# A planner-ordered decoder layer: other first loads, one-row products for a scale, two additions on GpSimd, and a new table of shifts

## The chip, the cores and the metric

The kernel runs on one core of one Trainium2 chip. The metric is the device time of one execution in microseconds (us). Three executions of the kernel before took 1163.86, 1164.89 and 1165.84 us, so the time before is their median, 1164.89 us.

The engines are named as in the profile: PE is TensorE (PEld its weight loads), DVE is VectorE, ACT is ScalarE, POOL is GpSimd, and SP is the queue of SyncE, from which nearly all transfers are started.

## The reference, cut to what matters

One decoder layer on a sequence of 1024 rows of width 1024, in float32. In shortened form:

```python
c_act = silu(c)
sh1, sc1, g1, sh2, sc2, g2 = split(c_act @ w_mod + b_mod, 6)   # six vectors of 1024
h = rms_norm(x, norm_mix_w) * (1 + sc1) + sh1
proj = h @ w_in                        # lx, ly (512 each), q, k, v, z (4 heads x 128 each), beta, alpha
# group 1: gated recurrence over lx, four blocks of 128 channels
xr = conv4(lx);  r, i = sigmoid(block products of xr)
h_lru = scan(a(r), sqrt(1 - a^2) * i * xr)
out_lru = rms_norm(h_lru * gelu(ly), lru_norm_w)      # needs the sum of squares over all four blocks
# group 2: gated delta rule, 4 heads, chunks of 64 rows
q, k, v = silu(conv4(q, k, v));  T = inverse(I + strict_lower(beta k k^T decay))
o = chunked recurrence;  out_gdn = rms_norm(o, gdn_norm_w) * silu(z)
x = x + g1 * (concat(out_lru, out_gdn) @ w_out)
h = rms_norm(x, norm_mlp_w) * (1 + sc2) + sh2
x = x + g2 * (square(relu(h @ w_up)) @ w_down)        # 1024 -> 4096 -> 1024
out = rms_norm(x, final_norm_w)
```

## The kernel before, in words

Every product that needs float32 exactness is done as three products of split operands: an operand is rounded to the type fp32r ("high"), the rest is kept in a second tile ("low"), and high x high, high x low and low x high are summed in PSUM (`mm3`, L596). Tiles are 128 partitions by 1024 columns (512 KB); 43 of them share the buffers of `big`. PSUM has 8 banks.

The work runs in stages, which the profile shows one behind the other.

1. **Start (0 to about 60 us).** The first loads are `x` (eight tiles `x0` to `x7`), the columns of `w_mod` that make the scale (`sc_w`), and the key columns of `w_in` (`wk`). `scale1(q)` (L864) makes a quarter of the scale, 256 of its 1024 values: eight blocks of `w_mod` are multiplied by the eight columns of `c_act` and added up, the first on ACT and seven on DVE (`macc`, L668), and PE then sums the 128 partitions with two products against a column of ones (tile `sc_c`). `xnorm(t)` (L833) normalises a row block of `x`. PE transposes it (`xTq`, `xTp`), ACT and DVE scale and split it into `hh` and `hl`, and the products for the four key heads follow (`first`, L797, tile `k_p`). The planner runs 36 products into a tile called `warm` (L900), which nobody reads.
2. **Projections z, q, v (to about 350 us)**, in three column groups of 342 each (`Proj.third`, L770), and beside them the keys' `LT` tiles, the triangular inverse, and the chunked recurrence of each head (`chain`, L1216).
3. **The inverse (`inverse`, L1064)**: a forward substitution of 31 steps on DVE, then `level1` (tiles `it` and `iy`, 32x32 products) and `level2` (tiles `iw` and `iz`, 64x64 products). Between `iy` and `iw`, DVE writes tile `aw`; `iw` needs it.
4. **Recurrence (about 300 to 465 us)**: `lx`, `ly` and `lru` (L1304), one block of 128 channels after the other. The low half of the convolved `xr`, tile `xrl`, is made in three steps: ACT rounds `xr` into `xrh`, ACT writes its negative into `xrl`, and a transfer issued from POOL's queue adds `xr` to it in memory (`GD`, the class `Adder`, L512). The `gate` products need `xrl`. The sum of squares over the four blocks, `msum`, is gathered in the same way: ACT squares a block into `lsq`, and a transfer from POOL's queue adds it to `msum`. The products `lrus` read `msum`.
5. **Output projection (tiles `wg`, `wl`), then the MLP**: `up` (tiles `upx`, `upy`, `upz`) and the down products (tile `dn`), to the end. The MLP uses seven products in place of eight.

What sets the order: nothing runs in the order of the source. A `Recorder` (L184) collects some 8370 operations, and `schedule` (L248) plays them once through a model of the engines with durations written in the code, and emits them in the order that comes out. Each engine and the SP queue then work in that fixed order. An operation's rank is `op.pri` (L258): for operations of the backbone (`rec.bb`) and all others it is the latest start that the model allows; for the early ones (`rec.early`) it is their place in the list. To this the planner adds a hand of tuned shifts: the table `SHIFTS` (L130) holds one small integer for each recorded operation, in quarters. In the early part the rank is therefore

```python
op.adj = SHIFTS[len(self.ops)] / 4.0
op.pri = i - 1e5 + op.adj      # early operations; lowest rank first
```

Operations with the bias `FILL` come last among those that are ready: PE takes one only when the model has nothing else for it. The model's durations for the small products of the inverse stand in L48: `L1A_DUR` 0.12 and `L1B_DUR` 0.2 us for one group of `level1`, `L2_DUR` 0.14 us for one of `level2`. A transfer that adds is modelled with `ADD_LAT` 1.8 us and 195 KB per us.

## Time and profile before

| what | value |
|---|---|
| median of three runs | 1164.89 us (1163.86 to 1165.84) |
| the profiled execution's own time | 1164.92 us |
| its span (first to last instruction) | 1162.9 us |
| mean granted TensorE clock | 0.984 |
| PE busy | 1129.3 us |
| DVE, ACT, POOL busy | 800.4, 635.3, 268.9 us |
| moved by the DMA engines | 250.03 MB |

How to read it: about 2 us of the time lie outside the span. The row by engine gives busy time; a busy PE says only that some product was in flight, so it has to be read beside the granted clock, which halves in places. The rows by stretch (one row for each stretch of time: its length, then the busy time and number of instructions of PE, PE's weight loads, DVE, ACT and POOL, then the granted clock, the share of the 16 DMA engines and their GB/s) show where that is. A row of the timeline gives start, duration, engine, line, operation, the tile written and the tiles read; the bracket is how long the engine had been idle and who ended that.

### The profile page before, as it was taken

How to read it: one execution, taken by the hardware profiler on the slowest of the kernel's cores; microseconds unless marked ns; L12 is line 12 of the kernel's file. 1: busy time of each engine (PE TensorE's matmuls, PEld its weight loads, DVE VectorE, ACT ScalarE, POOL GpSimd, SP SyncE). 2: the span in 40 equal slices, each digit the busy share in tenths (PEclk: the TensorE clock that was granted, in tenths of full speed). 3: DMA queues.
4: the chain of work that ended last, by engine and by line, in shares of the span. 5: the costliest groups of instructions: out<-in, count | busy, mean ns of one | idle time of the engine just before them, and what ended most of it. 6: DMA issues, size and time to landing. Idle time of an engine off the chain costs nothing.

```text
span 1162.9 us, 16590 instructions
## 1 busy us (share of the span) xinstructions
PE 1129.3 (97%) x6224; PEld 974.9 (84%) x6224; DVE 800.4 (69%) x1136; ACT 635.3 (55%) x982; POOL 268.9 (23%) x188
## 2 busy tenths in 40 slices
PE   5999997999998999899999999999999999999999
PEld 4889997899998987677888888887888888888888
DVE  7746799559767669757866666767675474974563
ACT  5746735454648895467655555556645343443341
POOL 2202210211211233200013121214500085723030
PEclk9999998699999999899999999999999999999999
DMA  9848955449667293522278777775999767774631
GB/s 335 263 112 256 295 174 170 140 124 275 193 170 211 65 295 107 168 82 87 91 253 276 242 252 265 241 236 202 387 390 402 272 211 272 269 252 132 227 134 73
DMA packets 135332, 250.03 MB, mean 215 GB/s; under 512 B 11282, under 2 KB 56527, under 8 KB 135251
## 3 DMA queue, kind: packets, MB, share of 16 engines
q1 hardware_dynamic: 130786, 232.71, 57.5%
q0 software_dynamic: 4464, 16.25, 7.3%
q8 instruction: 49, 0.80, 0.3%
q14 instruction: 33, 0.26, 0.1%
HBM read 173.93 MB, written 58.74 MB: 200 GB/s over the span
## 4 chain that ended last, share of the span: by engine, by line
PE 86%; DVE 5%; ACT 4%; DMA 3%; issue 2%; POOL 0%; SPq 0%; POOLq 0%; DVEq 0%; ACTq 0%
PE dn L414 27%; PE upx L414 15%; PE upz L414 8%; PE k_p L414 4%; PE z_p L414 4%; PE q_p L414 4%; PE upy L414 4%; PE wl L414 4%; PE v_p L414 3%; PE lx_p L414 2%; PE ch L414 2%; PE ly_p L414 2%; DVE xr L414 1%; PE cho L414 1%; DMA sc_w<-in_w_mod_dram 1%
## 5 line engine op out<-in xcount | busy, mean ns | idle before, releaser
L414 PE MATMUL upx<-h2h,U 128*128 128x512 f32 x512 | 167.8, 394 | 0.0
L414 PEld LDWEIGHTS upx<-h2h,U 128*128 128x128 f32 x512 | 96.2, 188 | 22.6
L414 PE MATMUL upx<-h2l,U 128*128 128x512 f32 x256 | 100.8, 394 | 0.0
L414 POOL TENSOR_TENSOR wd<-wd,wd 128x512 f32<-128x512 f32 x32 | 45.6, 1427 | 233.1 <-DMA wd<-in_w_down_dram 187.8
L414 ACT ACTIVATE act<-act 128x512 f32<-128x512 f32 x112 | 70.8, 633 | 51.1 <-DVE act L414 48.9
L414 DVE TENSOR_TENSOR U<-wu,U 128x512 fp32r<-128x512 f32 x112 | 78.1, 714 | 15.9 <-ACT U L414 15.8
L414 PE MATMUL upz<-h2h,U 128*128 128x512 f32 x256 | 85.0, 394 | 0.0
L414 ACT CAST U<-wu 128x512 fp32r<-128x512 f32 x112 | 66.7, 617 | 22.0 <-DVE wu L414 10.6
L414 DVE TENSOR_TENSOR act<-upz,ek 128x512 f32<-128x512 f32 x32 | 22.1, 691 | 55.9 <-PE upz L414 35.9
L414 PEld LDWEIGHTS upx<-h2l,U 128*128 128x128 f32 x256 | 48.1, 188 | 11.5
L414 PEld LDWEIGHTS upz<-h2h,U 128*128 128x128 f32 x256 | 48.1, 188 | 11.3
L414 ACT COPY ek<-upx 128x512 f32<-128x512 f32 x48 | 28.1, 586 | 53.5 <-PE upx L414 50.3
L414 PE MATMUL upz<-h2l,U 128*128 128x512 f32 x128 | 50.5, 395 | 0.0
L414 POOL TENSOR_TENSOR R<-R,R_5o 128x1024 f32<-128x1024 f32 x8 | 22.1, 2778 | 91.7 <-DVE keep L414 85.2
L414 PE MATMUL upy<-h2h,U 128*128 128x512 f32 x128 | 43.0, 394 | 0.0
L414 DVE TENSOR_TENSOR wu<-wu,wu 128x512 f32<-128x512 f32 x48 | 36.7, 779 | 0.0
L414 ACT ACTIVATE vn<-ch,bcoef 128x128 f32<-128x128 f32 x32 | 11.6, 366 | 44.1 <-PE ch L414 44.1
L414 PE MATMUL k_p<-hh,wkh 128*128 128x256 f32 (+2 forms) x104 | 30.9, 327 | 1.4 <-ACT hh L414 1.4
L414 PE MATMUL lx_p<-hl,lx_wh 128*128 128x342 f32 x96 | 32.1, 334 | 0.0
L414 PE MATMUL lx_p<-hh,lx_wl 128*128 128x342 f32 x96 | 32.0, 333 | 0.0
L414 PE MATMUL lx_p<-hh,lx_wh 128*128 128x342 f32 x96 | 31.7, 330 | 0.0
L414 PE MATMUL q_p<-hh,q_wl 128*128 128x342 f32 x96 | 31.5, 328 | 0.0
(578 smaller groups left out, 3578.8 us busy)
## 6 DMA issues: line engine op xcount, KB each, us to landing
L<-aod SPq DMA_DIRECT2D x56, 512.0 KB, 6.8
R<-in_w_down_dram SPq DMA_DIRECT2D x40, 512.0 KB, 6.1
wu<-in_w_up_dram SPq DMA_DIRECT2D x32, 512.0 KB, 4.0
aod<-as SPq DMA_DIRECT2D x64, 256.0 KB, 2.3
wd<-in_w_down_dram SPq DMA_DIRECT2D x32, 512.0 KB, 6.7
aod<-act SPq DMA_DIRECT2D x48, 256.0 KB, 2.2
sc_w<-in_w_mod_dram SPq DMA_DIRECT2D x16, 512.0 KB, 8.2
x<-in_x_dram SPq DMA_DIRECT2D x16, 512.0 KB, 6.3
```

The lines of the kernel that those rows point to most:

```text
L414: op.fn(*[res(v) for v in op.a], **{n: res(v) for n, v in op.k.items()})
```

## The change

The change has six parts.

1. **The first loads get another order.** In the source `x1` moves ahead of the second half of the first quarter of the scale, and the blocks for quarters two and three of the scale are loaded as four tiles of 512 columns (two quarters at once). Their final order on the SP queue comes from the new table (part 6).
2. **Part of the scale by one-row products.** Quarters 0 and 1 of the scale no longer use ACT and DVE: PE multiplies each of the eight columns of `c_act` (as a weight of one column) with a block of 256 columns and sums the eight in PSUM as one row (`sc1_r`); DVE copies the row, and PE turns it into two columns with two products against a single one. Quarters 2 and 3 become one pass of 512 columns in two groups of four blocks, one on ACT and three on DVE in each.
3. **The `warm` products move to the front.** The same 36, now `ones` by `ones`, are recorded first; the first of them has an early rank, and the other 35 keep the bias `FILL`.
4. **`xnorm`**: the scaling of `x2`, `x4` and `x6` moves from DVE to ACT.
5. **Two accumulating transfers become additions.** `xrl` is one subtraction `xr - xrh`, on GpSimd for blocks 0 to 2 and on DVE for block 3; `msum` is one addition on GpSimd for each of blocks 1 to 3.
6. **The order anew.** The model's durations for the small products of the inverse are 0.066 us (both kinds of `level1`) and 0.11 us (`level2`), and the whole table of shifts is another one. The old table has 8372 entries, 2394 of them not zero, the largest 75 places; the new one has 8364 entries, 3506 not zero, the largest 7112 places.

```diff
-FILL, WARM, AB_DUR, GATE_DUR, L1A_DUR, L1B_DUR, L2_DUR = 1e6, 36, 0.85, 0.89, 0.12, 0.2, 0.14
+FILL, WARM, AB_DUR, GATE_DUR, L1_DUR, L2_DUR = 1e6, 36, 0.85, 0.89, 0.066, 0.11
...
 _SHIFTS = (
...
     rec.early = True
+    warm = ps("warm0")
+    for i in range(WARM):
+        mm(warm[:, 0:P], ones, ones)
+        rec.ops[-1].bias = FILL if i else None
     crow = big("crow")[0:8, 0:P]
...
-    def load_sc1(q):
-        for a in range(2):
-            sc1_w[q, a] = w = v3(big(f"sc1_w{q}{a}"), 256)
-            SP.dma_start(out=w, in_=wm_p[:, 4 * a:4 * a + 4, D + q * 256:D + (q + 1) * 256])
+    def load_sc1(q, a):
+        n = 256 if q < 2 else 512
+        sc1_w[q, a] = w = v3(big(f"sc1_w{q}{a}"), n)
+        m = 1024 // n
+        SP.dma_start(out=w, in_=wm_p[:, m * a:m * a + m, D + q * 256:D + q * 256 + n])
...
     load_x(0)
-    load_sc1(0)
+    load_sc1(0, 0)
+    load_x(1)
+    load_sc1(0, 1)
     SP.dma_start(out=rows2[0:48, :], in_=b_mod.rearrange("a (r p) -> (a r) p", p=P))
...
-    load_x(1)
     load_wk(0)
     load_x(2, 3)
-    for q in range(1, 4):
-        load_sc1(q)
-        load_wk(q)
+    load_sc1(1, 0)
+    load_sc1(1, 1)
+    load_wk(1)
+    for a in range(4):
+        load_sc1(2, a)
+    load_wk(2)
+    load_wk(3)
     load_x(4, 5, 6, 7)
...
-        if t in (3, 5, 7):
+        if t > 1:
             A.mul(xt[t], xt[t], rs0[:, t:t + 1])
...
     def scale1(q):
-        acc = big(f"sc1_acc{q}")[:, 0:256]
-        for k in range(NK):
-            macc(acc, sc1_w[q, k // 4][:, k % 4, :], k)
+        n = 2 if q < 2 else 4
+        ks = slice(2 * q, 2 * q + n)
         pc = ps(f"sc1_c{q}")
-        for j in range(2):
-            mm(pc[:, j:j + 1], acc[:, j * P:(j + 1) * P], ones[:, 0:1])
-        ks = slice(2 * q, 2 * q + 2)
+        w = n * P
+        m = 1024 // w
+        if q < 2:
+            pr, row = ps(f"sc1_r{q}"), big(f"sc1_row{q}")[0:1, 0:w]
+            for k in range(NK):
+                mm(pr[0:1, 0:w], cact[:, k:k + 1], sc1_w[q, k // 4][:, k % 4, :], k == 0, k == NK - 1)
+            V.tensor_copy(row, pr[0:1, 0:w])
+            for j in range(n):
+                mm(pc[:, j:j + 1], row[:, j * P:(j + 1) * P], ones[0:1, 0:1])
+        for a in range(0 if q == 2 else 2, 2):
+            acc = big(f"sc1_acc{q}{a}")[:, 0:w]
+            for k in range(4):
+                wt, c = sc1_w[q, (4 * a + k) // m][:, (4 * a + k) % m, :], cact[:, 4 * a + k:4 * a + k + 1]
+                if k == 0:
+                    A.mul(acc, wt, c)
+                else:
+                    V.scalar_tensor_tensor(out=acc, in0=wt, scalar=c, in1=acc, op0=ALU.mult, op1=ALU.add)
+            for j in range(n):
+                mm(pc[:, j:j + 1], acc[:, j * P:(j + 1) * P], ones[:, 0:1], a == 0 and j == 0, a == 1, skip_group_check=True)
...
-    for q in range(1, 4):
-        scale1(q)
-        splitk(q, V if q == 1 else G)
+    scale1(2)
+    for q in (2, 3):
+        splitk(q, V)
...
-    warm = ps("warm")
-    for i in range(WARM):
-        mm(warm[:, i % 4 * P:i % 4 * P + P], ident, triu)
-        rec.ops[-1].bias = FILL
...
-                mms(L1A_DUR, [(p[blk[b + 1], c], LT[blk[b], i, blk[b + 1]], xnc[blk[b], i, :], True, True) for b in (0, 2)], 0.25)
+                mms(L1_DUR, [(p[blk[b + 1], c], LT[blk[b], i, blk[b + 1]], xnc[blk[b], i, :], True, True) for b in (0, 2)], 0.25)
...
         A.copy(xh, xr)
-        A.mul(xl_, xh.bitcast(F32), -1.0)
-        GD.dma_start(out=xl_.bitcast(F32), in_=xr)
+        (V if ct == 3 else G).tensor_tensor(out=xl_, in0=xr, in1=xh.bitcast(F32), op=ALU.subtract)
...
             A.activation(sq, yy, AF.Square)
-            GD.dma_start(out=msum, in_=sq)
+            G.tensor_tensor(out=msum, in0=msum, in1=sq, op=ALU.add)
```

104 lines of the change are left out of this document (77 added, 27 removed).

## The prediction

> **What bounds the kernel now.** I read the page first (busy time and the granted clock in 40 slices), then the stretches of time around each place where PE or its clock drops, then the waits of PE, then the timeline at those places.
>
> ```profile
> PE 1129.3 (97%) x6224; PEld 974.9 (84%) x6224; DVE 800.4 (69%) x1136; ACT 635.3 (55%) x982; POOL 268.9 (23%) x188
> PE   5999997999998999899999999999999999999999
> PEclk9999998699999999899999999999999999999999
> ```
>
> PE is the bound, but the first slice and slices 8 and 9 are holes, and in the latter the clock sags too. The stretches price the holes:
>
> ```profile
> 0.00:17.50 17.50, 3.40 (x13) 2.29 (x13) 10.51 (x32) 8.01 (x15) 2.25 (x10) 1.00 0.88 313
> 190.00:197.00 7.00, 5.24 (x313) 4.63 (x312) 6.85 (x9) 4.82 (x8) 0.00 (x0) 1.00 0.70 221
> 197.00:221.00 24.00, 17.73 (x143) 16.67 (x143) 17.12 (x19) 11.17 (x16) 3.71 (x2) 0.50 0.48 131
> 371.00:374.60 3.60, 1.80 (x11) 1.26 (x9) 3.60 (x3) 3.58 (x5) 0.00 (x0) 1.00 1.01 255
> 374.60:381.40 6.80, 5.22 (x20) 4.28 (x21) 3.55 (x4) 4.47 (x7) 0.86 (x1) 0.50 1.04 242
> 381.40:465.00 83.60, 83.60 (x439) 72.71 (x437) 65.79 (x59) 66.69 (x83) 25.07 (x16) 1.00 0.49 151
> 465.00:470.20 5.20, 0.89 (x9) 0.88 (x8) 4.69 (x3) 1.17 (x2) 2.90 (x2) 1.00 1.05 295
> 470.20:477.00 6.80, 6.80 (x22) 5.74 (x22) 3.11 (x5) 2.58 (x5) 3.31 (x2) 0.50 0.54 175
> 880.00:900.00 20.00, 20.00 (x88) 16.20 (x87) 9.70 (x9) 11.00 (x14) 0.00 (x0) 1.00 1.04 403
> 842.40:1153.80 311.40, 311.40 (x1347) 252.32 (x1346) 195.68 (x165) 130.54 (x157) 97.59 (x52) 1.00 0.68 244
> ```
>
> The last row shows the other kind of stage: the down products leave PE no idle time at full clock, so nothing is to be had there. Work done at half clock counts half. The inverse (190 to 221 us) loses 1.76 + 6.27 us of idle time and 17.73 / 2 = 8.87 us to the clock: 16.9 us. The gate hole (371 to 381.4) loses 1.80 + 1.58 + 5.22 / 2 = 6.0 us. The hole before `lrus` loses 4.31 + 6.80 / 2 = 7.7 us. What releases PE in them:
>
> ```profile
> PE lrus L414 <- DMA msum<-lsq: 4.3, 1, 4.3
> PE gate L592 <- DMA xrl<-xr: 3.4, 1, 3.4
> 197.35 3.92 DVE L414 SCALAR_TENSOR_TENSOR g_acc<-g_w,cact,g_acc 128x1024 f32<-128x1024 f32 x3
> 199.51 0.24 PE L592 MATMUL iy<-ttc,xtc 32*32 32x32 f32 x1
> 204.89 1.28 DVE L414 SCALAR_TENSOR_TENSOR aw<-iy,bcoef 32x512 f32<-32x512 f32 x2
> 205.72 0.55 PE L592 MATMUL iw<-aw,LT 64*64 64x64 f32 x3 [3.86 <-DVE aw L414]
> ```
>
> The first two are the transfers that the change replaces. In the inverse the last `iy` product starts at 199.51, but DVE writes `aw` only at 204.89, because its fixed queue has `g_acc` and other work ahead; PE's queue stands behind `iw`.
>
> **The start.** An early load's rank is its place plus its table entry. Worked out with the old table this gives `c`, a norm weight, three blocks of `sc_w`, two small rows, `x0`, `x1`, `wk0`, which is what the SP queue of this profile shows (the rows for `sc_w` and `x` below). With the new table it gives `sc_w` 01, `c`, `sc_w` 00, `sc_w` 11, `x1`, `x3`, `x2`, `x0`, `sc_w` 10, three small rows, `wk0`, `wk1`. Of the 512 KB loads `x0` moves from the 4th to the 7th place and `wk0` from the 6th to the 9th.
>
> ```profile
> 1.53 1.50 SPq L414 DMA_DIRECT2D sc_w<-in_w_mod_dram  x3
> 4.03 0.83 SPq L414 DMA_DIRECT2D x<-in_x_dram  x2
> 5.42 0.51 ACT L414 ACTIVATE sc_acc<-sc_w,cact 128x256 f32<-128x256 f32 x1 [2.36 <-DMA sc_w<-in_w_mod_dram]
> 10.34 1.06 ACT L414 ACTIVATE xj<-x 128x1024 f32<-128x1024 f32 x1 [3.02 <-DMA x<-in_x_dram]
> 13.13 0.62 ACT L414 CAST wkh<-wk 128x512 fp32r<-128x512 f32 x1 [0.35 <-DMA wk<-in_w_in_dram]
> 15.93 1.06 ACT L414 ACTIVATE xj<-x 128x1024 f32<-128x1024 f32 x1 [0.21 <-DMA x<-in_x_dram]
> 17.49 1.01 PE L414 MATMUL k_p<-hh,wkh 128*128 128x256 f32 x3 [1.40 <-ACT hh L414]
> 17.50:22.40 4.90, 4.90 (x23) 4.90 (x24) 4.44 (x11) 3.66 (x6) 1.27 (x2) 1.00 1.07 375
> ```
>
> The 1st, 4th, 6th and 8th load landed at 5.42, 10.34, 13.13 and 15.93, so 1.4 to 1.6 us each. The 7th lands near 14.7, the 9th near 17.3. From the last load it needed, `wk0`, to the first key product the old path took 17.49 - 13.13 = 4.4 us. In the new order `x0` plus as much gives 19.1, and `wk0` lies between 17.3 + 0.62 (the cast alone) = 17.9 and 17.3 + 4.4 = 21.7. I take 18.9, near the first, since by then only the cast is left: 1.4 us later than before. But it starts at full clock if the `warm` products hold it: 36 of them cost 8.0 us warm (row below) and 16 cold, inside the 14.1 us that PE idles before 17.5. In the old order the 4.90 us after 17.5 were worth 2.45; from 18.9 to 22.4 at full clock are 3.5. Gain 1.0 us.
>
> The rest of the start hangs on that idle time. A one-row product over 256 columns is shown nowhere. Nearest row: one `warm` product over 128 columns is two instructions, 8.04 us for 36, or 0.22 us; twice the columns give 0.45 us, 16 of them 7.1 us. From below, 0.12 us for 256 columns in the rounded type; from above 0.9 us at half clock. I take 0.45, and cost it at nothing: quarter 0 and `sc_w` 11, 10 land (near 8 and 16 us) before `wk0`, so PE has nothing else. If that cover is gone, quarter 1 costs 3.6 us of PE. On DVE 28 sums of 0.485 us (median, row further down) go, six on 512 columns come, between that and the 1.3 us of `g_acc` on 1024, and two splits move there from POOL; three scalings of `x` go to ACT: all beside PE, which is bound from 22.4 on. Ends for the start: +3.5 (2.45 by the clock alone, plus 1.0 for a first product at 17.9) and -5 us (3.6, plus one load of 1.4 late).
>
> **The inverse.** The planner believed in 16 x 2 groups of 0.12 + 0.2 us and 64 of 0.14, and filled DVE's queue for that. With 0.066 and 0.11 it will put `aw` right after `iy`. That takes 204.89 - 199.7 = 5.2 us out; the 1.76 us of idle before 197 can be filled with projections. Of the 8.87 us lost to the clock I take half, 4.4, since the small products themselves leave little for the clock to see. 11 us; ends 0 and 16.9. Late next is `iw` behind ACT and DVE copies of 0.6 us.
>
> The Trainium skill (TensorE: Matmul & The Clock Gate, What's actually happening) says that the clock falls only after a whole idle window of about 3.4 us; by that rule filling the gap saves all 8.87 us and the sum below would be 1138.5. Here the clock fell at 197 although PE was busy for 5.24 of the 7 us before, with 32x32 products, so I stay with half.
>
> **`xrl` and `msum`.**
>
> ```profile
> 365.69 1.05 ACT L414 ACTIVATE xrl<-xrh 128x1024 fp32r<-128x1024 f32 x1
> 367.04 0.92 POOL L414 DMA_DIRECT2D xrl<-xr  x1 [9.18 <-ACT xrl L414]
> 24.02 2.42 POOL L414 TENSOR_TENSOR wkl<-wk,wkh 128x1024 fp32r<-128x1024 f32 x1 [4.32 <-ACT wkh L414]
> L414 DVE SCALAR_TENSOR_TENSOR sc_acc<-sc_w,cact,sc_acc x35: 473/485/2345, 6.0 to 289.4; 128x256 f32<-128x256 f32 x28, 128x1024 f32<-128x1024 f32 x7
> 24.38 2.35 DVE L414 SCALAR_TENSOR_TENSOR sc_acc<-sc_w,cact,sc_acc 128x256 f32<-128x256 f32 x1
> 376.18 2.50 PE gate L592 x10
> 462.33 0.88 POOL L414 DMA_DIRECT2D msum<-lsq  x1 [6.45 <-ACT lsq L414]
> 462.60 6.40 DVE L414 SCALAR_TENSOR_TENSOR wo<-wo,cols,g_bc 128x1024 f32<-128x1024 f32 x1
> 469.35 2.79 PE lrus L414 x16
> 470.11 1.23 DVE L414 TENSOR_TENSOR wo1l<-wo,wo1h 128x1024 fp32r<-128x1024 f32 x1 [0.51 <-ACT wo1h L414]
> ```
>
> For block 1 of `xrl`, ACT's negative (1.05), the issue (0.92) and the transfer end when `gate` starts, at 376.2. A subtraction on POOL takes 2.42 us and can start where ACT's negative started: ready near 368.1, before PE ran dry at 371. Four ACT instructions and seven transfers of 512 KB go; three plus three POOL operations of 2.42 us and one of DVE of 1.2 us come, and the two weight transfers that POOL issues between them can wait up to 1.5 us longer each, hidden as long as PE has projections queued. I take 5.5 of 6.0 us. For `msum`, ready at 462.3 + 2.4 = 464.7 instead of 469.3. But late next is `wo1l`, which the third block of the first `wl` tile needs and which ends at 471.3 in the old order, because DVE's product on 1024 columns (1.3 us by `g_acc`) took 6.40 beside two POOL operations. I take 4 of 7.7 us. Ends for both together: 13.7 and -4 (six POOL operations hold DVE for 14.5 us; 65.79 of 83.6 us are taken, which leaves 17.8).
>
> **The end.**
>
> ```profile
> L414 PE MATMUL warm<-triu,ident x72: 272/275/275, 1153.6 to 1161.6; 128*128 128x128 f32 x72
> 1153.80 8.04 PE warm L414 x72
> SPq L1807 <- PEq L1807: 0.7, 2, 0.5
> ```
>
> The old `warm` products run after the last real product, to 1161.84, and the final synchronisation waits 0.5 us for PE. They go to the front: 0.5 us, ends 0 and 0.7 (both waits of the row).
>
> Sum: 1.0 + 11 + 5.5 + 4 + 0.5 = 22.0 us. Against the profiled execution's own 1164.92 us (span 1162.9 plus 2.0 around it; the median of the runs is 0.03 us lower) that is 1142.9; I say 1143. All upper ends together are 34.8 us: 1130.
>
> **The rivals.**
> *DVE becomes the bound of the recurrence.* POOL's 2.42 us beside a DVE sum that took 2.35 instead of 0.485 us says that DVE stands still. If the six additions hit the last block's chain, the 9.5 us of `gate` and `lrus` go: 1152.5. Against it: 17.8 us of room. The Trainium skill (SBUF — State Buffer, Who interferes with whom) has this as a rule: the shared port pair is locked for a whole instruction and the other side blocks. The trace agrees (2.35 us).
> *The change doesn't do what it says in the inverse.* DVE is at 6.85 of 7 us and 17.12 of 24; if it, not the order, is the limit, 11 us go: 1154.
> *Slower: the new order brings the MLP's loads late.* The table changes all ranks, and around 880 to 900 us the DMA engines are full (1.04, 403 GB/s) while PE never waits. Each load of 512 KB that falls behind there costs 512 / 403 = 1.3 us once PE has caught up. From 17 late loads on this eats the 22 us; with 24 it is 1174. For it: no slack can be read from a PE that never waits. Against it: the planner models this queue, and in the old order it held.
>
> **How the numbers follow.** The likeliest case (0.56) gives 1143, its own range 1134 to 1151. The DVE case has 0.12, the inverse case 0.11, the slower one 0.18, and 0.03 is left for gains and losses that cancel. Faster by over 0.2% (2.3 us, about what a measurement of this kernel can tell from no change): 0.56 + 0.12 + 0.11 = 0.79; within 0.03; slower 0.18. The range goes from the sum of the upper ends, 1130, to just short of no change, 1164, and leaves out the slower case.
>
> **What would show it.** Right: key products at full clock before 20 us; `iw` within 2 us of the last `iy`; no half clock near `gate` and `lrus`; no `warm` at the end. Wrong: `wk0` or `x0` still awaited after 19 us; DVE products of 2 us and more beside POOL's in the last `lru` block and PE waiting for `lrus` or `wl`; PE waits for loads in `dn`; a half-clock stretch at a new place.

## The result and the profile after

The changed kernel takes 1164.03 us (median of 12 executions, 1162.17 to 1167.40), the kernel before, run beside it, 1164.97 (12 executions, 1163.01 to 1167.33). The ratio is 0.9989, with an interval of 0.9978 to 1.0000: no difference that can be measured. The forecast of 1143 was wrong, and 1164.03 lies just outside its range of 1130 to 1164. The profiled execution took 1164.57 us, its span is 1162.8.

The same rows of the page as before: busy time, and PE and its clock in 40 slices.

```profile
PE 1133.3 (97%) x6264; PEld 968.2 (83%) x6264; DVE 801.0 (69%) x1114; ACT 628.8 (54%) x979; POOL 287.4 (25%) x185
...
PE   6999899999999999999999999999999999999997
...
PEclk9999999999999999999999999999999999999999
```

The sag of the clock in the seventh and eighth slice (counted from one; the prediction calls them 8 and 9) is gone, and so are the `warm` products at the end (the last slice is a 7). The fifth slice shows an 8 that was not there. The stretches say more (columns as in the prediction): first the changed kernel, then the kernel before at two places where it had no hole.

```profile
104.00:129.30 25.30, 20.30 (x151) 19.71 (x150) 14.58 (x23) 16.93 (x39) 4.46 (x5) 0.93 0.95 270
186.00:226.00 40.00, 40.00 (x424) 37.38 (x424) 23.83 (x36) 19.25 (x30) 3.41 (x3) 1.00 0.45 134
226.00:240.00 14.00, 10.70 (x64) 10.41 (x63) 7.70 (x11) 4.35 (x7) 0.69 (x1) 0.88 0.77 215
365.00:392.00 27.00, 26.82 (x178) 26.06 (x179) 21.78 (x26) 25.37 (x34) 5.79 (x4) 1.00 0.80 256
470.00:477.00 7.00, 6.77 (x34) 5.44 (x33) 3.19 (x4) 1.68 (x4) 6.51 (x3) 0.86 0.73 225
```
```profile
104.00:129.30 25.30, 25.30 (x171) 25.28 (x170) 16.49 (x26) 18.54 (x40) 3.11 (x3) 1.00 0.97 316
226.00:240.00 14.00, 14.00 (x112) 14.00 (x110) 5.70 (x18) 5.09 (x11) 0.40 (x1) 1.00 0.25 76
```

All three holes that the prediction priced are closed as waits: PE is busy for 40.00 of 40 us at full clock through the inverse, and for nearly all of the time around `gate` and `lrus`. Right behind `lrus` the clock still halves for 3.4 us from 474.97 on (the 0.86 in the row 470.00:477.00; in the kernel before it was 6.8 us). But there are new holes, at 104 to 129 us (the key stage: `ktok`, `kk` and the first `z_p`) and at 226 to 240 us. PE's waits name them:

```profile
PE q_p L458 <- DMA q_wl<-q_w: 5.4, 2, 3.3
...
PE ktok L458 <- DVE LT L458: 3.1, 1, 3.1
...
PE z_p L458 <- DMA z_wl<-z_w: 1.6, 1, 1.6
```
```profile
L458 PE MATMUL warm<-ones 128*128 128x128 f32 x46 | 7.7, 296 | 0.0
```

The second fence is the group of `warm` products between 104 and 129.3 us of the changed kernel. The stage looks busier than it is: 7.7 of its 20.30 busy us are products that nobody reads.

**Where the time went.** To compare two kernels that do the same work in another order, I lay PE's products of each in order of time, count each with its start-to-start time at full clock (0.23 us for 512 columns, less for fewer), leave out `warm`, the scale's products and the small transposes, and read when each kernel has done the same sum. The table gives how far a kernel is ahead of the one before (negative: behind), at the time that the kernel before shows. e8, e9, e17 and e18 are experiments below.

| time in before, us | what lies before it | after | e8 | e9 | e17 | e18 |
|---|---|---|---|---|---|---|
| 61 | start | -5.0 | -5.1 | -1.0 | -5.1 | -5.1 |
| 123 | key stage | -18.9 | -13.0 | -1.0 | -13.0 | -13.8 |
| 183 | `z_p`, forward substitution | -23.3 | -17.4 | -1.0 | -17.3 | -30.8 |
| 219 | inverse | -7.0 | -1.1 | 12.6 | -1.1 | -14.6 |
| 240 | first `q_wl` wait | -10.9 | -6.2 | 1.8 | -1.2 | -14.7 |
| 363 | other `q_wl` waits | -15.0 | -9.8 | 1.8 | -2.3 | -15.7 |
| 389 | `gate` | -8.8 | -3.8 | 2.6 | 3.8 | -9.6 |
| 542 | `lrus`, `wl` | -0.8 | 5.8 | 3.6 | 13.2 | 0.2 |
| 1152 | MLP | -1.2 | 5.6 | 3.1 | 13.2 | -1.6 |

The rows at 183, 219 and 363 lie amid small products and depend on what these are counted at. With each shape's median distance in the kernel before they read -19.8, -6.2 and -16.6 for the changed kernel, and 10.0 for e9 at 219; the other rows move by 0.2 us or less.

In the changed kernel the three holes gave 16.3 (inverse), 6.1 (`gate`) and 8.0 us (`lrus` and `wl`). Of the 8.0, 5.9 came by 480 us; the rest came from 500 us on, where PE's waits for `h2r` shrank from 2.7 to 0.8 us. The start cost 5.0, the key stage 13.9, the stretch before the inverse 4.4 and the stretch of the `q_wl` waits 8.0 (219 to 363 us in the table). The MLP cost 0.4, and after the last real product it gained 1.2, since no `warm` tail follows. That is 31.6 us gained and 31.7 lost, the case of "gains and losses that cancel" to which the prediction gave 0.03. By the other count the inverse gave 13.6 and `gate` 7.8, the stretch before the inverse cost 0.8 and that of the `q_wl` waits 10.4; the balance is the same.

### The profile page after: what moved, and what is told of

Its sections match the earlier page's. It is cut to its first block, busy times and chain, and to the rows that moved or that the text cites. A ratio compares the mean times of both kernels' runs of the same rounds, so it can differ in the third digit from the quotient of the medians.

```text
span 1162.8 us, 16592 instructions
## 1 busy us (share of the span) xinstructions
PE 1133.3 (97%) x6264; PEld 968.2 (83%) x6264; DVE 801.0 (69%) x1114; ACT 628.8 (54%) x979; POOL 287.4 (25%) x185
## 4 chain that ended last, share of the span: by engine, by line
PE 88%; DMA 5%; issue 3%; DVE 1%; ACT 1%; POOL 1%; SPq 0%; POOLq 0%; ACTq 0%
PE dn L458 26%; PE upx L458 15%; PE upz L458 8%; PE wl L458 4%; PE lx_p L458 4%; PE q_p L458 4%; PE ly_p L458 4%; PE upy L458 4%; PE wg L458 3%; PE k_p L458 3%; PE z_p L458 3%; DMA q_wl<-q_w 2%; PE ch L458 1%; PE v_p L458 1%; DMA sc_w<-in_w_mod_dram 1%
## 5 line engine op out<-in xcount | busy, mean ns | idle before, releaser
L458 POOL TENSOR_TENSOR wd<-wd,wd 128x512 f32<-128x512 f32 x32 | 50.0, 1569 | 287.8 <-DMA wd<-in_w_down_dram 123.2
L458 DVE TENSOR_TENSOR U<-wu,U 128x512 fp32r<-128x512 f32 x112 | 83.3, 762 | 21.6 <-ACT U L458 21.0
L458 PE MATMUL q_p<-hh,q_wl 128*128 128x342 f32 x96 | 31.6, 329 | 5.4 <-DMA q_wl<-q_w 5.4
L458 PE MATMUL q_p<-hl,q_wh 128*128 128x342 f32 x96 | 32.3, 337 | 0.0
L458 PE MATMUL z_p<-hh,z_wl 128*128 128x342 f32 x96 | 30.8, 320 | 1.6 <-DMA z_wl<-z_w 1.6
L458 PE MATMUL q_p<-hh,q_wh 128*128 128x342 f32 x96 | 32.2, 336 | 0.0
L458 PE MATMUL v_p<-hl,v_wh 128*128 128x342 f32 x96 | 31.9, 333 | 0.0
```

The costliest lines, as they stand in the source:

```text
L458: op.fn(*[res(v) for v in op.a], **{n: res(v) for n, v in op.k.items()})
```

## The experiments

Most change the order alone; e1, e5, e7 and e18 also change operations, and e10, e11 and e16 leave out `warm` products. A list of moves is applied to the order that the planner has finished: `(engine, tiles, (engine2, tile2, n))` takes the operations of an engine that write these tiles, or a slice of them, and puts them just ahead of the n-th operation that writes tile2. Tiles carry the kernel's own numbers here, which the profile's names leave out. Ratios are to the kernel before, with their 95% interval.

### Is part 5 worth its 9.5 us by itself? (e1, e5)

e1 is the kernel before, with its own order, and the two accumulating transfers as additions.

```diff
         A.mul(xl_, xh.bitcast(F32), -1.0)          # left out
-        GD.dma_start(out=xl_.bitcast(F32), in_=xr)
+        (V if ct == 3 else G).tensor_tensor(out=xl_, in0=xr, in1=xh.bitcast(F32), op=ALU.subtract)
-            GD.dma_start(out=msum, in_=sq)
+            G.tensor_tensor(out=msum, in0=msum, in1=sq, op=ALU.add)
```

> The kernel before with its own order on every queue, and only part 5 put in: the three transfers-with-add for xrl and msum become additions at the same place of POOL's queue (block 3 of xrl on DVE). Theory A (the two waits go and nothing takes their place; in the trace of after, PE gained 6.1 us about gate and 5.7 us about lrus): 1153 us, range 1151 to 1158. Theory B (POOL's additions hold DVE through shared operands, the rival of the prediction): 1161 to 1168 us, with DVE operations of 2 us and more beside POOL's.

Measured: 1162.58 us, ratio 0.9982 [0.9972, 0.9992]. The `gate` hole gave 5.9 us, and the rest was taken back: the wait for `lrus` shrank, but PE then stood for `wo0l`, and the clock was at half from 464.5 to 474.8 us. PE's waits between 355 and 480 us:

```profile
PE wl L414 <- POOL wo0l L414: 4.6, 1, 4.6
PE wg L414 <- POOL gcl L414: 2.2, 3, 1.2
PE lrus L414 <- POOL msum L414: 1.1, 1, 1.1
```

`wo0l` and `gcl` are other work of POOL, now behind the additions in its queue. Their slot is longer than forecast, too: the three additions to `msum` took 2.86 us on average and the three of `xrl` 3.11, against the 2.42 of the prediction. e5 takes POOL's queue out of the way:

```diff
+    ('POOL', 'wo0l wo2l', ('POOL', 'msum', 2)),
+    ('POOL', 'msum:0-1', ('POOL', 'xrl3', 0)),
```

> As the additions alone (e1), and two changes in the order of POOL's queue: wo0l and wo2l ahead of the last msum addition, the first msum addition behind the four gcl. In e1 the waits for xrl and msum went (gate 5.9 us earlier, lrus 3.7), and PE then stood 2.2 us for gcl and 4.6 us for wo0l, which POOL worked off behind the new additions. Theory A (the additions are worth 8 to 10 us, and POOL's order takes them back): 1154 to 1158 us. Theory B (POOL's additions slow DVE, whose operations beside them took 2 to 3.4 us in e1 in place of 1.2, and DVE is late next): 1160 to 1163 us.

Measured: 1162.80 us, 0.9981 [0.9972, 0.9991], no better. The waits for `gcl` and `wo0l` are gone, and DVE is late instead. First PE's waits of e5, then rows of its timeline, then the same scan in e1.

```profile
PE lrus L441 <- POOL msum L441: 3.6, 1, 3.6
PE wg L441 <- DVE x L441: 2.1, 1, 2.1
```
```profile
453.50 3.42 POOL L441 TENSOR_TENSOR wo0l<-wo,wo0h 128x1024 fp32r<-128x1024 f32 x1
456.88 4.39 POOL L441 TENSOR_TENSOR wo2l<-wo,wo2h 128x1024 fp32r<-128x1024 f32 x1
454.54 4.52 DVE L441 TENSOR_TENSOR_SCAN xr<-aa,xr 128x1024 f32<-128x1024 f32 x1
```
```profile
454.69 2.28 DVE L414 TENSOR_TENSOR_SCAN xr<-aa,xr 128x1024 f32<-128x1024 f32 x1
```

The scan took twice as long, not beside one of the new additions but beside `wo0l` and `wo2l`, which e5 had moved there; `lsq`, and with it the last addition to `msum`, came late. So e1 lost its gain to POOL's queue, and e5 lost it because DVE stands still beside POOL, which is the mechanism of the rival "DVE becomes the bound of the recurrence", with other work of POOL's in the part of the additions. In these two orders part 5 by itself is worth 2 us, not 9.5. In the changed kernel the same additions gave 6.1 us about `gate` and 5.9 about `lrus`, under another order of POOL's and DVE's queues.

### Does `aw` right after `iy` fill the inverse? (e2, e6, e9)

e2 is the kernel before with `aw` ahead of the four `g_acc` and two `v1T` that stood before it on DVE; e6 also moves ACT's `g_h` and `v_wh` and POOL's `g_l` behind the copies of `aw`.

```diff
+    ('DVE', 'g1_acc:2-6', ('DVE', 'g1_acc', 6)),     # e2 and e6
+    ('DVE', 'v1T:0-2', ('DVE', 'g1_acc', 6)),        # e2 and e6
+    ('ACT', 'g1_h v2_wh', ('ACT', 'v1th', 0)),       # e6 alone
+    ('POOL', 'g1_l', ('ACT', 'v1th', 0)),            # e6 alone
```

> The kernel before, and only DVE's queue changed at one place: four sums into g_acc and two steps of v1T are put behind the two writes of aw, which so follow the last iy. Theory A (aw is what iw waits for, and the half clock after it is the wait's consequence): between 5 us (the wait of 3.86 us and a little) and 14 us (with the half clock) faster, 1151 to 1160 us, iw within 2 us of aw. Theory B (behind aw the next late thing, the copies of iz on DVE, eats it): 1163 to 1166 us.

> As e2 (aw first on DVE), and on ACT the rounding of g_acc and of v_w, with POOL's low half of g_acc, behind the three copies of aw from iw. In e2 aw came 5 us earlier and PE's iw too, but ACT stood 8.4 us for g_acc ahead of those copies, and PE waited 4.0 us for them. Theory A (the inverse has two late steps in a row, on two queues): 5 to 9 us faster than before, 1156 to 1160 us. Theory B (a third step is late right behind): 1163 to 1165 us.

Measured: 1164.85 us, 1.0006 [0.9994, 1.0019], and 1165.22 us, 1.0003 [0.9992, 1.0013]. Nothing. Rows of the timeline of e2, then one stretch of e2 and of e6:

```profile
198.93 0.21 PE L619 MATMUL iy<-ttc,xtc 32*32 32x32 f32 x1 [3.01 <-issue]
...
199.93 1.28 DVE L441 SCALAR_TENSOR_TENSOR aw<-iy,bcoef 32x512 f32<-32x512 f32 x2 [2.99 <-ACT LT L441]
```
```profile
197.00:221.00 24.00, 18.04 (x144) 16.89 (x143) 16.78 (x18) 10.57 (x16) 3.73 (x2) 0.51 0.42 121
```
```profile
197.00:221.00 24.00, 18.32 (x179) 17.07 (x169) 18.73 (x19) 11.67 (x16) 3.73 (x2) 0.50 0.42 128
```

`aw` came 4.96 us earlier, at 199.93, as forecast. But the clock is at half from 197 to 221 all the same, and by 213 us `iz` waits as long as `iw` had. So the step "`aw` right after `iy` takes 5.2 us out" is wrong as a cause. e9 tests the other reading: PE fed with large products through the whole inverse.

```diff
+    ... the four moves of e6, and
+    ('PE', 'q2_p2:5-8', ('PE', 'iy0', 3)),
...
+    ('PE', 'q2_p2:20-24', ('PE', 'iy1', 10)),
+    ('PE', 'q2_p0:0-4', ('PE', 'iy0', 14)),
+    ('PE', 'q2_p0:4-12', ('PE', 'iw1', 0)),
```

> Before, with aw ahead on DVE and its neighbours (as in the run before this) and with products of q2_p2 and q2_p0 put between the groups of iy and around iw, so that PE has large products all through the inverse. Theory (what the changed kernel gained in the inverse came from keeping PE busy there, not from aw): the granted clock stays at 1.00 from 190 to 221 us, the stretch costs 8 to 14 us less than before, the time is 1151 to 1157 us. Rival (the clock falls there whatever PE is fed): half clock from about 197 to 219 again and a time of 1162 to 1166 us.

Measured: 1162.81 us, 0.9984 [0.9974, 0.9994]. The stretches and the wait that decides:

```profile
190.00:197.00 7.00, 7.00 (x209) 5.79 (x207) 6.83 (x9) 5.18 (x8) 0.00 (x0) 1.00 0.67 217
197.00:211.50 14.50, 14.44 (x273) 12.70 (x271) 9.78 (x10) 5.67 (x9) 0.00 (x0) 1.00 0.31 103
211.50:221.00 9.50, 2.51 (x13) 2.54 (x13) 8.95 (x10) 6.04 (x7) 3.73 (x2) 0.69 0.59 180
```
```profile
218.49 0.45 PE L452 MATMUL vtok<-ident,v1T 128*128 128x128 f32 x1 [7.05 <-DVE v1T L452]
```

Fed, PE keeps its full clock up to 211.5 us, and the inverse gains 13.6 us (the table: from -1.0 to 12.6; 11.0 by the other count). That is the theory's half. Then 10.8 us (8.2) are given back: PE runs dry for 7.05 us on `v1T`, because DVE's nine `g_acc` and `v1T` are no faster than they were (8.95 of 9.50 us busy), and the clock falls there. So both halves of the inverse's price, idle time and clock, go when PE is fed, and DVE's work must be out of the way as well. The changed kernel has both: in the stretch of 186 to 226 us its DVE is busy for 23.83 of 40, and all seven `g_acc` start at 221.96 us or later, behind the last `iz` product (205.51), where the kernel before starts them from 192.97 to 206.20, amid the inverse.

### The key stage (e3, e8, e10, e11)

Rows of SP's and POOL's timeline in the changed kernel, then those of the kernel before that answer to them:

```profile
88.73 6.27 SPq L458 DMA_DIRECT2D z_w<-in_w_in_dram  x2
...
96.81 2.63 POOL L458 TENSOR_TENSOR rnk<-ssk,mhalf 128x8 f32<-128x8 f32 x1 [10.00 <-DVE ssk L458]
99.42 0.90 POOL L458 DMA_DIRECT2D z_wl<-z_w  x1
103.11 3.52 POOL L458 DMA_DIRECT2D k_dm<-gdr  x4 [2.78 <-DMA gdr<-gT]
```
```profile
50.20 1.00 SPq L414 DMA_DIRECT2D z_w<-in_w_in_dram  x2
...
89.89 2.66 POOL L414 DMA_DIRECT2D k_dm<-gdr  x3 [11.23 <-DMA gdr<-gT]
```

The new order loads the last three of the four `z_w` blocks 38 to 43 us later, and starts the adding transfers of `k_dm` behind `rnk` and `z_wl`, all four in one burst; the first three start 13 us later. Before, 143 `z_p` products filled the stretch of 104 to 129.3 us; now 33 lie there, and `warm` runs. e3 and e8 load `z_w` early; e3 puts 48 `z_p` products in two lumps ahead of `ktok`, e8 puts the `k_dm` additions ahead of `rnk` and leaves PE's order alone.

```diff
+    ('SP', 'z0_w z1_w z2_w z3_w', ('SP', 'k3_dm', 0)),           # e3 and e8
+    ('PE', 'gT', ('DVE', 'k1T', 1)),                             # e3 and e8
+    ('DVE', 'gT', ('DVE', 'k1T', 1)),                            # e3 and e8
+    ('ACT', 'z0_wh z0_wl z1_wh z1_wl', ('ACT', 'k0_st', 2)),     # e3 and e8
+    ('POOL', 'z0_wl z1_wl', ('ACT', 'k0_st', 2)),                # e3 and e8
+    ('POOL', 'k0_dm k2_dm k3_dm k1_dm', ('POOL', 'rnk', 0)),     # e8 alone
+    ('PE', 'z1_p0', ('PE', 'ktok3_1', 0)),                       # e3 alone, with
+    ('PE', 'z1_p1', ('PE', 'ktok1_0', 0)),                       # z2's split ahead
```

> The changed kernel with its own order, and only the key stage moved: the four loads of z_w ahead of the first k_dm on the SP queue (about 60 us, where the DMA engines stand idle), the transpose and copy of gT one and a half steps of k1T earlier, the splits of z0, z1 and z2 ahead on ACT and POOL, and the 48 products z1_p0 and z1_p1 ahead of two sets of ktok transposes on PE. Theory A (the loads and adding transfers that come late and together made the hole of some 14 us between 100 and 130 us): 8 to 14 us faster than the change, 1150 to 1156 us. Theory B (the hole is made elsewhere, or what it gave comes back as a wait in the later projections): 1161 to 1165 us.

> The changed kernel with its own order, and in the key stage only what feeds it: the z_w loads at 60 us, gT earlier, z0 and z1 split earlier, and the four adding transfers to k_dm ahead of the small rnk on POOL. PE's order stays. Theory A (late feeding made the hole): 6 to 12 us faster, 1152 to 1158 us. Theory B (PE's own order has nothing to do there but the short products of the key stage, each of which waits for DVE or ACT, so that earlier feeding moves it a little): 0 to 4 us faster, 1160 to 1164 us.

Measured: e3 1168.51 us, 1.0031 [1.0016, 1.0046]; e8 1159.91 us, 0.9957 [0.9942, 0.9972], 4.1 us faster than the changed kernel. In e8, a row of the timeline and the stretch:

```profile
94.84 3.57 POOL L489 DMA_DIRECT2D k_dm<-gdr  x4 [20.45 <-DMA gdr<-gT]
```
```profile
104.00:129.30 25.30, 24.74 (x190) 24.32 (x190) 16.89 (x34) 21.18 (x47) 5.88 (x4) 1.00 0.87 276
```

The additions start 8.3 us earlier and the stage loses 7.9 us where it lost 13.9. In e3 they still started behind `rnk`, at 100.73, and the stage lost as much as in the changed kernel; that its lumps delayed the chain of `ktok`, DVE and ACT is likely and not shown. Which of e8's moves carries how much was not separated, and the 7.9 us that stay are not explained: PE's order holds 72 `z_p` products there where the kernel before has 143. Two runs look at the rest: e10 feeds the stage with small pieces of `z_p` in place of `warm`, e11 leaves out all `warm` products from the ninth on.

```diff
+    ... the moves of e8, and in e10
+    ('ACT', 'z2_wh z2_wl', ('ACT', 'z0_st', 0)), ('ACT', 'z3_wh z3_wl', ('ACT', 'k2th', 0)),
+    ('PE', 'z1_p0:0-8', ('PE', 'ktok3_1', 0)), ('PE', 'z1_p0:8-16', ('PE', 'kk3_1', 0)),
...
+    ('PE', 'z1_p1:20-24', ('PE', 'kk3_0', 0)),
+        gone = set(ops_of("PE", "warm0")[8:])          # e10 and e11
```

> After, with the earlier z_w loads and k_dm additions of the last run, the splits z2 and z3 earlier too, and 48 products of z1_p0 and z1_p1 in small pieces between the key products where the warm products stood; no warm product is left from the ninth on. Theory (with the loads there, the rest of the key stage's hole is PE work that could have run: feed): another 3 to 6 us against the last run, 1154 to 1157 us. Rival (the chain of ktok, DVE and ACT sets the stage, whatever PE is fed): z_p resumes at 122 to 124 us with less left to do or the chain is delayed by as much as is fed in; 1159 to 1162 us.

> The last run's earlier loads and additions, and no warm product from the ninth on, nothing in their place. Theory A (the warm products cost PE time there, since they stand in its fixed queue): 46 fewer instructions between 104 and 123 us make the stage up to 5 us shorter, 1155 to 1158 us. Theory B (PE waits for the chain anyway, warm or not): within 1 us of 1160. Theory C (warm holds the clock): the granted clock falls between 104 and 123 us and the time is 1162 us or more.

Measured: e10 1160.14 us, 0.9948 [0.9927, 0.9970]; e11 1157.44 us (1155.36 to 1162.95), 0.9938 [0.9919, 0.9957]. The intervals overlap with that of e8, so neither is shown to be faster. In e10, PE was 3.3 us further on at 123 us than in e8, and lost it at the next place, where the forward substitution on DVE sets the time:

```profile
PE it L682 <- DVE xnc L504: 3.2, 1, 3.2
```

In e11 the clock fell in the stage (first row) and in the profiled execution, the slowest of six, again in the inverse (second row):

```profile
104.00:129.30 25.30, 21.45 (x144) 20.42 (x143) 16.92 (x35) 21.99 (x50) 6.42 (x5) 0.93 0.90 282
180.00:210.00 30.00, 29.32 (x238) 25.56 (x231) 13.37 (x19) 10.29 (x15) 3.23 (x2) 0.66 0.32 91
```

Without `warm` PE waits for the same chain, at a lower clock. Whether `warm` costs time there stays open: five of e11's six executions took 1155.36 to 1158.35 us, below e8's median of 1159.91, its own median lies in the range of its theory A, and its profiled execution was 0.9 us ahead of e8's at 123 us.

### The start (e4, e7, e12, e13, e18)

In the changed kernel no `warm` product ran in the start (first at 37.5 us), and the first key product came at 22.49 us, not at 18.9:

```profile
7.11 4.54 PE L458 MATMUL sc_r<-sc_w,cact 128*1 128x256 f32 x12 [2.12 <-DMA sc_w<-in_w_mod_dram]
...
13.49 1.02 PE L458 MATMUL sc_r<-sc_w,cact 128*1 128x256 f32 x4
...
15.08 1.04 ACT L458 ACTIVATE xj<-x 128x1024 f32<-128x1024 f32 x1
...
22.49 0.50 PE L458 MATMUL k_p<-hh,wkh 128*128 128x256 f32 x2
```

The ACT row is the square of `x0`, the last of four, though the first key products need `x0` and `x1` alone. A one-row product is two instructions (32 for 16 products). They start 0.43 us apart up to 10.5 us and 0.22 us apart after that, where the granted clock is 1.00 from 10.76 us on. Each of the five runs tries one suspect or more.

e4 moves the 36 `warm` products ahead of the first key product:

```diff
+    ('PE', 'warm0:0-6', ('PE', 'crow_ps', 0)),
...
+    ('PE', 'warm0:32-36', ('PE', 'k0_p0', 0)),
```

> The changed kernel with its own order, and only the 36 warm products moved on PE: 10 ahead of the first one-row product, 6 between the one-row products, the rest ahead of the transposes and the first key product, all before 22 us. Theory A (the start lost 4 us because PE stood at half clock while it worked off the one-row products, and the warm products were not there): the full clock before 15 us, the first key products 2 to 4 us earlier, 1159 to 1162 us. Theory B (the loads set the start, or the clock falls again before 22 us): within 1 us of the change, 1163 to 1165 us. Theory C (warm products in the key stage cost PE time that is now free): a gain at 100 to 130 us, not at the start.

Measured: 1168.39 us, 1.0033 [1.0019, 1.0046]. The clock was full from 12.05 us on, no earlier than without `warm` in front: four one-row instructions at 8.00 us, behind 20 instructions of `warm`, still started 0.42 us apart, and eight at 12.39 0.22 apart, as in the changed kernel. And a `warm` product stands in PE's fixed queue like any other: the first key product came at 27.24 us.

e7 is the changed kernel without one-row products: the same places in the order, the sums on ACT and DVE. e12 moves `x0` ahead on SP, ACT, DVE and POOL.

```diff
-                mm(pr[0:1, 0:w], cact[:, k:k + 1], sc1_w[q, k // 4][:, k % 4, :], k == 0, k == NK - 1)
+                # k == 0: acc = w * c on ACT; others: acc = w * c + acc on DVE            (e7, e18)
+    ('SP', 'x0', ('SP', 'x1', 0)), ('ACT', 'xj0', ('ACT', 'xj1', 0)),                  # e12
+    ('DVE', 'x0', ('DVE', 'x1', 0)), ('PE', 'xTq0_0', ('PE', 'xTq0_1', 0)),            # e12
...
```

> The changed kernel with its own order, and part 2 undone for the first two quarters of the scale: at the places of the sixteen one-row products on PE, ACT and DVE form the weighted sums as the kernel before does, and PE's two products against a column of ones follow. Theory A (the one-row products took 0.26 us of PE for each of 32 passes, warm or not, and stood in PE's queue ahead of the first key products): the start 3 to 5 us earlier, 1159 to 1161 us. Theory B (the order of the first loads, x0 eighth and wk0 thirteenth, sets the start): within 1 us of the change, 1163 to 1165 us.

> After, with the load of x0 ahead of x1, ACT's square of x0 and the scaling behind it ahead of those of x1, x3 and x2, and the first split of hh and hl ahead. Theory (the start's 5 us come from x0 standing fourth of the x loads and of ACT's squares): the first key product moves from 22.5 to 19 to 21 us, and 1 to 3 us stay to the end, 1161 to 1163 us. Rival (wk0 and the scale's last products set it, or the gain waits at the key stage): first key product 21 to 22.5 us and a time of 1163.5 to 1165 us.

Measured: e7 1178.50 us, 1.0121 [1.0093, 1.0148]; e12 1168.19 us, 1.0014 [0.9998, 1.0031]. In e7 the first key product came only 0.7 us earlier, so the one-row products alone are not the cause. They also had a use: without them the full clock came at 24.23 us, in the changed kernel at 10.76. Most of its 14.5 us come from elsewhere: the clock fell in the inverse (a row of the timeline, then the stretch).

```profile
189.69 0.44 PE L458 MATMUL qtok<-ident,q0T 128*128 128x128 f32 x2 [2.19 <-issue]
```
```profile
190.00:218.00 28.00, 28.00 (x212) 24.02 (x211) 11.81 (x15) 9.28 (x13) 3.23 (x2) 0.57 0.22 57
```

In e12 the first key product came at 27.26 us: PE's queue still had `x1`'s transpose ahead of the last one-row passes, so that PE waited 3.09 us for it, and the clock then stood at half from 14.1 to 24.3 us. e13 reorders all queues of the start for the first 24 key products.

```diff
+    ('SP', 'x0 rows2 wk0', ('SP', 'x3', 0)),
+    ('ACT', 'xj0 wkh0:0-1', ('ACT', 'xj3', 0)), ('DVE', 'bcol A1:0-2', ('DVE', 'rs0', 2)),
+    ('PE', 'sc1_r0 sc1_c0 xTq0_0:1-3', ('PE', 'xTp4_0', 0)),
+    ('PE', 'k0_p0:0-2', ('PE', 'xTq0_1', 0)),
...
```

> After, with the start in the order in which the first 24 key products need it: the loads of x0, the small rows and wk0 ahead of x3; the scale's first quarter, its column form and A ahead of the transposes; x0 ahead of x3 and x2 on ACT, DVE and POOL; the 24 products ahead of the transposes of x3 and x2 and of the second quarter's one-row products. Theory (the start's 4 us come from the fixed queues' order, x3, x2 and the second quarter standing ahead of what the first products need): first key product at 16 to 18.5 us in place of 22.5, 2 to 4 us of it left after 60 us, time 1160 to 1162.5 us. Rival (the later x3, x2 and second quarter take it back within the first 30 us, or the key stage swallows it): at 60 us no more than 1 us gained, time 1163.5 to 1165 us.

Measured: 1167.31 us, 1.0029 [1.0016, 1.0041].

```profile
8.09 6.17 PE L516 MATMUL sc_r<-sc_w,cact 128*1 128x256 f32 x16 [3.24 <-DMA sc_w<-in_w_mod_dram]
...
19.00 0.58 PE L516 MATMUL k_p<-hh,wkh 128*128 128x256 f32 x1 [0.56 <-ACT hh L516]
...
24.64 0.59 PE L516 MATMUL sc_r<-sc_w,cact 128*1 128x256 f32 x2
...
31.48 0.62 PE L516 MATMUL k_p<-hh,wkh 128*128 128x256 f32 x3
```

The first key product came 3.5 us earlier, but at half clock (0.50 from 16.7 to 23.5 us); and from 24.3 to 31.5 us the second quarter's passes and the transposes now stand in front of the next ones, and at 61 us the kernel is 9.9 us behind, worse than the changed kernel's 5.0. e14 puts this start and e8's key stage together:

```diff
+    ... the moves of e8 and of e13
```

> The last run's start and the earlier z_w loads and k_dm additions of run e8 together. Theory (two separate losses, which add up): 4.1 us of e8 and what e13 gained, 1156 to 1158 us. Rival (the key stage is bound by the chain behind the loads, so that PE is only earlier at the same wait): 1159 to 1161 us, as e8.

Measured: 1162.90 us, 0.9991 [0.9978, 1.0003]: 3.0 us slower than e8, for a start that is 3.3 us later at 61 us (-8.4 against -5.1). So nearly all of the loss in the start is paid at the end here; in e13 it was 3.3 of 4.9 us (against the changed kernel).

### The `q_wl` waits, and all together (e15 to e18)

The low half of `q_w` goes the way of `xrl` before the change: ACT's negative, then an adding transfer from POOL's queue. In the changed kernel one such transfer started at 225.84 and PE waited for it at 234.72; in e17 it starts at 199.37, and `q_wl` is not among PE's waits.

```profile
225.84 0.85 POOL L458 DMA_DIRECT2D q_wl<-q_w  x1 [27.76 <-ACT q_wl L458]
...
234.72 0.43 PE L458 MATMUL q_p<-hh,q_wl 128*128 128x342 f32 x1 [3.31 <-DMA q_wl<-q_w]
```
```profile
199.37 0.86 POOL L494 DMA_DIRECT2D q_wl<-q_w  x1 [7.20 <-ACT q_wl L494]
```

```diff
+    ('ACT', 'q2_wh q2_wl', ('ACT', 'vn0_0', 0)), ('POOL', 'q2_wl', ('ACT', 'vn0_0', 0)),
+    ('ACT', 'q3_wh q3_wl', ('ACT', 'g1_h', 0)), ('POOL', 'q3_wl', ('ACT', 'g1_h', 0)),
+    # e15: with the moves of e14; e16: the same without warm from the ninth on
+    # e17: with the moves of e8; e18: e17 with the sums of e7 and a start as in e13
```

> The same, with ACT's split of q2_w and q3_w and the adding transfers of q2_wl and q3_wl earlier, ahead of other work of ACT and POOL. Theory (PE's waits for q_wl, 5.0 us in e8, are paid in full): 3 to 5 us faster than e14, 1152 to 1155 us. Rival (ACT's other work, moved behind, is late next): within 1.5 us of e14.

> The same as e15 without warm products from the ninth on. If they only filled idle time and held the clock: no faster than e15, and in some executions 5 to 7 us slower, since the clock falls in the inverse or the key stage. If they cost PE time in its queue: 1 to 3 us faster than e15.

> After, with the earlier z_w loads and k_dm additions (as e8) and the earlier q2_wl and q3_wl (as e15), and the start as it is in after. Theory (the losses are separate and add up): e8's 1159.9 less the 4.4 us by which e15 was ahead of e14, 1155 to 1156.5 us. Rival (the q_wl waits were longer only because of the other start): 1158.5 to 1160.5 us.

> The same as e17, with the scale's quarters 0 and 1 by ACT and DVE as in before (no one-row products; same output) and the start in the order of what the first key products need. Theory A (the one-row products cost PE time in the start that nothing hides: 32 passes of 0.26 to 0.39 us): the first key product at 16.5 to 18.5 us, and the start's loss falls from 4 to 5 us at 60 us to 0 to 1.5 us; if the clock holds in the inverse, 1150 to 1153 us. Theory B (DVE's sums or the loads are as late, whatever computes the scale): the first key product after 20 us or 3 to 5 us of loss at 60 us all the same; 1155 us or more. If the clock falls in the inverse, as in e7, the time is 5 to 13 us longer, and the loss at 60 us decides alone.

Measured:

| run | us | ratio to before |
|---|---|---|
| e15 | 1157.38 (1155.38 to 1158.15) | 0.9940 [0.9928, 0.9953] |
| e16 | 1157.39 (1155.28 to 1168.87) | 0.9952 [0.9930, 0.9974] |
| e17 | 1150.63 (1150.10 to 1152.40) | 0.9878 [0.9862, 0.9893] |
| e18 | 1166.23 (1162.30 to 1168.70) | 1.0004 [0.9992, 1.0017] |

e15 is 5.5 us faster than e14, and e17 9.3 us faster than e8, by the same four moves. e17 beats both kernels: 14.5 us less than the one before, 13.4 less than the changed one. Its stretch at the first `q_wl` wait, where the changed kernel had 10.70 us and 0.88:

```profile
226.00:240.00 14.00, 13.21 (x98) 12.96 (x96) 10.83 (x14) 9.33 (x13) 1.16 (x2) 1.00 0.51 144
```

PE's waits for `q_wl` were 5.0 us in e8, and 7.5 of its 8.7 us in that part of the table are gone in e17: after the wait the clock is down, too (0.76 between 226 and 240 us in e8). e16 hints at what `warm` is for: two of its twelve executions took 1166.99 and 1168.87 us at a mean clock of 0.984 and 0.981, the others 1155 to 1158 at 0.992 to 0.994. That `warm` prevents this is not shown: e15 ran only five times, and e12, which keeps all of `warm`, ranges from 1160.70 us at 0.995 to 1169.32 at 0.988.

e18 was to settle the start and did not, though it shows more. Its first key product came at 17.29 us, as early as before, and it is as far behind at 61 us as e17, because the next group waits (two rows of the timeline, then a stretch in the inverse):

```profile
17.29 0.58 PE L534 MATMUL k_p<-hh,wkh 128*128 128x256 f32 x1 [0.96 <-ACT hh L534]
...
26.96 0.62 PE L534 MATMUL k_p<-hh,wkh 128*128 128x256 f32 x3 [2.21 <-ACT hh L534]
```
```profile
187.50:210.00 22.50, 22.50 (x153) 19.23 (x152) 8.95 (x13) 7.64 (x12) 3.24 (x2) 0.50 0.26 71
```

By the reckoning of the table e18 is level with the kernel before at 24 us; then PE waits for an `hh` that ACT starts only at 26.45, behind a cast of `wkh` and two products for the later quarters of the scale (from 24.28 on). That puts it 2.8 us behind, and the rest is lost by 55 us. In the changed kernel PE has no idle time there: transposes and one-row passes stand in front of the key products. So two things make the start late at about the same time, and no run here took both away. Which of the moved loads or scalings carries the second one stays open. The last row is the clock again: at 183 us in the table e18 is 13.5 us further behind than e17, and the two end 15.6 us apart.

## Why the prediction was wrong, point by point

**Start (forecast +1.0, measured -5.0).** Two premises failed. `warm` was to hold the clock from the front, but only the first has an early rank, and the trace shows none before 37.5 us; the first key products ran at full clock all the same, since the one-row passes had brought it by 10.76 us. (That the kernel before had half clock after 17.5 us is right, though the row says 1.00: its clock is on record from 23.04 us on, and its key products start 0.21 us apart before that and 0.12 after.) And the start was taken to end with `wk0` (18.9 us); it ended with `x0`'s chain and the one-row passes, at 22.49. The price of a one-row product was right (0.45 us taken, and 0.9 at half clock; two instructions measured 0.43 and 0.86), but "cost it at nothing" was not: 20 of the 32 instructions ran after 13.4 us, between other work. The lower end of -5 was met, but by luck: its 3.6 us were the one-row products of quarter 1, and without any of them (e7) the kernel is still 4.5 us behind at 61 us.

**Inverse (forecast +11, measured +16.3, or 11.9 with the 4.4 us that the new order spent just before it).** The size was right, the cause was not: `aw` alone gave nothing (e2, e6). Feeding PE gave 11.0 to 13.6 us (e9), since it keeps the clock; the changed kernel also moved `g_acc` out of DVE's way. Half of the clock's 8.87 us was taken; all of it went. That is what the rule of the Trainium skill (TensorE: Matmul & The Clock Gate, What's actually happening) had for this term, though the total that it gave, 1138.5, missed the same losses as mine.

**`xrl` and `msum` (forecast +5.5 and +4, measured +6.1 and +5.9; 2.1 more came behind `lrus`, in no term of the sum).** Right in the changed kernel, and the waits are gone. But it is not the additions alone that do it: in the old order they are worth 2 us. What takes the rest is POOL's queue in e1, which the prediction had at 2.42 us for an addition (up to 3.43 measured) and at 1.5 us, hidden, for what stands behind it; and in e5 DVE standing still beside POOL, the rival's mechanism.

**End (forecast +0.5, measured +1.2).** Right in kind, above its upper end of 0.7.

**What was missing.** The sum had a term for every hole that goes and none for holes that come. The key stage's 13.9 us and the 8.0 of the `q_wl` stretch are together as much as the whole gain that was forecast. e8 and e17 show them as loads and adding transfers that the new order starts too late: repaired, 13.4 us come back (1164.03 to 1150.63), 5.9 of the key stage's and 7.5 of the other; what else the key stage loses is open. The third rival had the mechanism, "the new order brings loads late", and put it in the MLP, where PE lost 0.4 us. It was wrong on the place, because it looked where the DMA engines are full; the places that lost were those where a short chain of a load, a split and an adding transfer feeds PE.

Of the signs named for it, no half clock near `gate` and no `warm` at the end came true; `iw` came 1.2 us after `iy` in the first half and 3.6 in the second; 3.4 us of half clock near `lrus` remained, and the key products did not come before 20 us. Of the signs against it, the half-clock stretch at a new place came (0.93 at 104 to 129 us, 0.88 at 226 to 240), and it pointed at the two stages that lost most.

## What to carry to other kernels

When a change reorders everything, the holes in the old profile bound the gain and say nothing of the loss: list, for each stage that PE runs through without a wait, the transfers that feed it and their slack in the old order, and ask of the new order where each of them stands in its queue. A hole of 3 us is not worth 3 us: ask whether the clock falls in it. And a filler product in a fixed queue is free only where the queue would have waited anyway.

## What the runs showed of the hardware

- PE pauses for 1.2 to 3.9 us after a dense run of 32x32 products, with nothing that the profile shows to wait for ("issue": 1.17 and 3.01 us in the kernel before, 1.62 and 3.92 in e6, 2.19 in e7). In the 2 us ahead of the longest, 128 such products had started, in e7 60. It was not tried what causes it.
- The clock can fall without such a pause being long. In the kernel before it fell at 197.12 us, 0.7 us into the pause of 3.01; in e6 at 196.98, before its pause of 3.92 began at 197.56. In the 3.3 to 3.4 us ahead of the fall PE was busy for 1.55 us there, for 1.68 in e6, 1.71 in e7 and 2.72 in e11. The Trainium skill (TensorE: Matmul & The Clock Gate, What's actually happening) names an idle window of about 3.4 us as what throttles. By these rows less idle time than that is enough.
- In the inverse the clock then stays at half for 20 to 24 us, even where PE is never idle (e18: 22.50 of 22.50 us busy at 0.50, the work there being 64x64 and 32x32 products with 25 large ones of `q_p` and 12 of `qk` between them). Elsewhere, as at 374.6 us in the kernel before, it was back after 6.8 us. What makes the difference was not tried.
- Whether it falls is not settled by the order of the work alone. e7 and the changed kernel have the same order there and are equally late at 123 us (19.0 and 18.9 us); the one pauses and loses its clock, the other does neither. And e11 and e16 have executions of one and the same kernel at a mean clock of 0.994 and of 0.981 to 0.988, 6 to 12 us apart.
